# The last layer norm of a decoder layer, moved beside the last expert of a mixture of experts

## The chip, the cores and the metric

The kernel runs on one core of a Trainium2 chip. The metric is the device time of one execution in microseconds (us), lower is better. Every time of the profile below comes from one profiled execution, and its clock starts with that execution's first instruction.

## The reference

One decoder layer over 1024 tokens of width 1024, all float32. The first half (windowed attention, a convolution branch, a gated merge, a layer norm) is not touched by the change. What follows it is:

```
h     = layer_norm(alpha * x + mix)                       # 1024 x 1024
logits = h @ w_router + b_router;  top 4 of 32 experts, softmax over the 4
for each chosen expert e:  up = h @ w_up[e] + b_up[e]      # 1024 -> 2048
    act = min(up[::2],7) * sigmoid(1.702*...) * (clip(up[1::2],-7,7) + 1)
    y_moe += gate * (act @ w_down[e] + b_down[e])          # 1024 -> 1024
out   = layer_norm(alpha * h + y_moe) * ln2_g + ln2_b
```

## The kernel before

**Experts.** The 32 experts are ranked by their number of tokens. Rank j has a fixed capacity `CAPS[j]` (320 slots for rank 0, 256 for rank 5, 64 for ranks 25 to 31). Tokens above a capacity go to a list that a loop at the end works off, in chunks of 128 (`nxv` chunks; with these inputs there are none). Two DRAM tensors hold the state of a token: `hd` has h, and `yd` starts as alpha*h plus the gated b_down and collects the experts' rows. An expert gathers its rows of `hd` by index, and scatters its gated result into `yd` with an indirect DMA that adds (`scatter`, line 319, on GpSimd's queue). Two scatters are never in flight at once, since both write `yd`.

**Blocks.** A capacity is cut in blocks of 128 slots, and one of 64 or 32. For a 128-block every float32 product is three matmuls over high and low parts (line 251), and the weights are split into these parts on ScalarE and VectorE (`split`, lines 86 and 87). For a block of 64 slots, 64 columns of the array serve each half of the outputs (line 260): its result lies as 128 partitions x 512, in which slot t has its first 512 channels in partition t and the others in partition 64 + t. `si` holds the row index of such half rows.

**Steps and pairs.** An expert takes 12 steps: 0 to 3 and 4 to 7 are the two halves of the up projection, 8 to 11 the down projection. Each step needs 1 MB of weights, loaded on SP's queue into 24 slots of 512 KB; a planner (`fits`) issues a load as soon as the slots allow. The experts are taken in pairs, and the two of a pair alternate by phases of four steps. The last pair is rank 5 (256 slots, tiles named `p5...`) and rank 25 (64 slots, `p25...`). The order of the steps is the list G:

```
G = [(e, 4 * ph + s) for pair in pairs for ph in range(3) for e in pair for s in range(4)]
```

What goes with a step (transposes, SwiGLU, bias, scatter, gathers) is entered in a table with `at(step, function)`, and `behind(g)` issues it after the matmuls of step g, in a fixed order of kinds. Each engine works off its instructions in the order in which they were issued. Accumulators in PSUM come from 5 buffers; a 128-block needs two of them in a phase, a 64-block one.

**The end.** After the last step come the remaining entries of the table, then the loop over overflow chunks (`nxv`, lines 1328 and 1329), and then the last layer norm: eight tiles `fy` of 128 tokens are loaded from `yd` on SP's queue (line 1358), and for each one VectorE takes statistics (`fst`, `fmv`), ScalarE a square root, and the normalisation is shared between VectorE (line 1377), ScalarE (1381) and GpSimd (1382):

```
nc.vector.scalar_tensor_tensor(y[:, cs], y[:, cs], mv[:, 0:1], LG2[0][:, cs], op0=ALU.subtract, op1=ALU.mult)
if b == NB - 1 or c == 1:
    nc.vector.scalar_tensor_tensor(y[:, cs], y[:, cs], rstd, LG2[1][:, cs], op0=ALU.mult, op1=ALU.add)
else:
    nc.scalar.activation(y[:, cs], y[:, cs], AF.Copy, scale=rstd)
    nc.gpsimd.tensor_tensor(y[:, cs], y[:, cs], LG2[1][:, cs], op=ALU.add)
```

Of the kernel before, what the change touches and what calls it, by code (L numbers as in the profile page):

```python
# [53 lines left out]
PAIRS = [(6, 31), (1, 30), (13, 19), (2, 29), (9, 14), (7, 20), (21, 22), (0, 28), (15, 23), (3, 27), (10, 16), (8, 24),  # L54
         (11, 17), (4, 26), (12, 18), (5, 25)]
TR = 9 * P


@with_exitstack
def kernel(ctx: ExitStack, tc: tile.TileContext, x, w_in, b_in, attn_sinks, w_attn_br,  # L60
# [36 lines left out]
    def trp(name):  # L97
        return ps.tile([P, 512], F32, name=name, tag="tr", bufs=3)
# [1079 lines left out]
    with tc.manual_schedule():  # L1178
        NS = 12
        pairs = [(ex[n], ex[n + 1]) for n in range(0, NE, 2)]  # L1180
        G = [(e, 4 * ph + s) for pair in pairs for ph in range(3) for e in pair for s in range(4)]
        total = len(G)
        pos = {(e.pfx, s): g for g, (e, s) in enumerate(G)}

# [38 lines left out]
        def overflow():  # L1223
# [12 lines left out]
            for d in (1, 2, 4, 8, 16):  # L1236
# [19 lines left out]
            nc.sync.dma_start(xti[:, :], xci)  # L1256


        todo = {}

        rank_of = ("x_T", "swiglus", "act_T", "scale_out", "bias_of", "scatter", "fetch", "indices", "gather", "load_row",
                   "load_bias")

        def at(g, f, *a):
            todo.setdefault(g, []).append((f, a))
# [2 lines left out]
        g0 = {e.pfx: pos[e.pfx, 0] for e in ex}  # L1268
        tpos = [g0[e.pfx] - 2 - e.nb + i for e, i in blocks]
        for n, e in enumerate(ex):  # L1270
            p = g0[e.pfx] - 4 * (n % 2)
            if n > 1:
                at(p - 16, e.fetch)
                at(p - 13, e.indices)
# [8 lines left out]
            for i in range(e.nb):  # L1283
                at(pos[e.pfx, 4 + i], e.act_T, 0, i)
                at(pos[e.pfx, 8 + (i > 0)], e.act_T, 1, i)
                at(pos[e.pfx, 11], e.scale_out, i)
            at(pos[e.pfx, 11] + 2, e.scatter)
        for n, (e, i) in enumerate(blocks):
            if n >= XG:
                f = g0[e.pfx] // 24 * 24  # L1290
# [26 lines left out]
        for g, (e, s) in enumerate(G):  # L1317
# [3 lines left out]
                overflow()  # L1321
            load_ahead(g)
            behind(g)
        for g in sorted(todo):
            behind(g)


    nxv = nc.values_load(nxi[0:1, 0:1], min_val=0, max_val=NPX)  # L1328
    with tc.For_i(0, nxv, 1) as it:  # L1329
        xe = mo.tile([1, 2], I32, name="xe", tag="xe")  # L1330
        nc.sync.dma_start(xe, xti[bass.ds(it, 1), :])
        ev = {n: n.value_load(xe[0:1, 0:1], min_val=0, max_val=NE - 1) for n in (nc.sync, nc.gpsimd)}
        row = nc.gpsimd.value_load(xe[0:1, 1:2], min_val=0, max_val=NE * TR - P)
        idx = [mo.tile([P, 4, 2], F32, name="xm", tag="xm"), mo.tile([P, 4], I32, name="xgi", tag="xgi"), None]
        e = Expert("x", P, lambda eng=nc.sync: ev[eng], idx, fast=False)
        e.fetch(row)
        e.indices()
        e.gather(0)
        e.x_T(0)
        for s in range(12):  # L1340
            e.load(s)
            e.mm(s)
            if s in (3, 7):
                for u in (s // 2 - 1, s // 2):
                    e.load_row(u)
                    e.bias_of(u)
                e.swiglus(s // 4)
                e.act_T(s // 4, 0)
        e.scale_out(0)
        e.scatter()  # L1350


    mctx.close()
    fin = ctx.enter_context(tc.tile_pool(name="fin", bufs=2, reuse_waits="tile"))
    FY, LG2 = [], []
    for b in range(NB):
        FY.append(fin.tile([P, D], F32, name=f"fy{b}", tag="fy", bufs=8))
        nc.sync.dma_start(FY[b], yd[b * P:(b + 1) * P, :])
        if b < 2:
            row = fin.tile([1, D], F32, name=f"l2row{b}", tag=f"l2row{b}", bufs=1)  # L1360
            nc.scalar.dma_start(row, (ln2_g, ln2_b)[b])
            bc = fin.tile([P, D], F32, name=f"l2bc{b}", tag=f"l2bc{b}", bufs=1)
            nc.gpsimd.partition_broadcast(bc, row)
            LG2.append(bc)
    for b in range(NB):
        y = FY[b]
        mv = fin.tile([P, 2], F32, name=f"fmv{b}", tag="fmv")
        st = fin.tile([P, 2, 6], F32, name=f"fst{b}", tag="fst")
        for h in range(2):
            nc.vector.bn_stats(st[:, h, :], y[:, h * 512:(h + 1) * 512])  # L1370
        nc.vector.bn_aggr(mv, st)  # L1371
        rstd = fin.tile([P, 1], F32, name=f"frs{b}", tag="frs")
        nc.scalar.activation(rstd, mv[:, 1:2], AF.Sqrt, bias=eps_t)  # L1373
        nc.vector.reciprocal(rstd, rstd)  # L1374
        for c in range(2) if b >= NB - 2 else (None,):
            cs = slice(None) if c is None else slice(c * 512, (c + 1) * 512)
            nc.vector.scalar_tensor_tensor(y[:, cs], y[:, cs], mv[:, 0:1], LG2[0][:, cs], op0=ALU.subtract, op1=ALU.mult)  # L1377
            if b == NB - 1 or c == 1:
                nc.vector.scalar_tensor_tensor(y[:, cs], y[:, cs], rstd, LG2[1][:, cs], op0=ALU.mult, op1=ALU.add)  # L1379
            else:  # L1380
                nc.scalar.activation(y[:, cs], y[:, cs], AF.Copy, scale=rstd)  # L1381
                nc.gpsimd.tensor_tensor(y[:, cs], y[:, cs], LG2[1][:, cs], op=ALU.add)  # L1382
            (nc.scalar if b % 2 else nc.sync).dma_start(out[b * P:(b + 1) * P, cs], y[:, cs])  # L1383


_INS = ['x', 'w_in', 'b_in', 'attn_sinks', 'w_attn_br', 'conv_w', 'conv_b', 'conv_ln_g', 'conv_ln_b', 'w_conv_br',
# [25 lines left out]
```

## Time and profile before

| | us |
|---|---|
| median of 3 runs | 2189.25 (2187.02 to 2190.99) |
| the profiled execution | 2188.17 |
| its span, first to last instruction | 2186.6 |
| matmuls of the last pair, first to last | 2038.3 to 2129.4 |
| loop over overflow chunks left | 2139.9 |
| last layer norm on VectorE | 2143.65 to 2177.8 |

The span and the time of the execution differ by 1.57 us. The mean granted clock of TensorE is 0.976 of full speed; the stretch after the last matmul has most of what is missing.

### The profile page before, as it was taken

How to read it: one execution, taken by the hardware profiler on the slowest of the kernel's cores; microseconds unless marked ns; L12 is line 12 of the kernel's file. 1: busy time of each engine (PE TensorE's matmuls, PEld its weight loads, DVE VectorE, ACT ScalarE, POOL GpSimd, SP SyncE). 2: the span in 40 equal slices, each digit the busy share in tenths (PEclk: the TensorE clock that was granted, in tenths of full speed). 3: DMA queues.
4: the chain of work that ended last, by engine and by line, in shares of the span. 5: the costliest groups of instructions: out<-in, count | busy, mean ns of one | idle time of the engine just before them, and what ended most of it. 6: DMA issues, size and time to landing. Idle time of an engine off the chain costs nothing. (4 is left out here: it accounts for less than half of the span.)

```text
span 2186.6 us, 31962 instructions
## 1 busy us (share of the span) xinstructions
PE 2069.1 (95%) x10925; PEld 1370.3 (63%) x10925; DVE 1377.5 (63%) x2052; ACT 878.9 (40%) x1337; POOL 496.8 (23%) x643
## 2 busy tenths in 40 slices
PE   8999999999959999999999999989999999999990
PEld 7776788887635566576654355556676466766760
DVE  3768799665845564656964126365596569569635
ACT  3155511432323433435653123334455357356521
POOL 1000000003332222323241322122243241232204
PEclk9999999999979999999999999999999999999995
DMA  5111112142339988998998997899889898988944
GB/s 161 41 37 30 30 49 58 34 139 64 107 116 326 313 289 301 362 347 266 319 312 296 345 333 259 283 335 328 281 312 285 307 305 303 357 259 314 346 161 162
DMA packets 191096, 506.92 MB, mean 232 GB/s; under 512 B 34700, under 2 KB 70974, under 8 KB 190929
## 3 DMA queue, kind: packets, MB, share of 16 engines
q1 hardware_dynamic: 163062, 448.86, 57.9%
q0 software_dynamic: 26592, 52.21, 9.9%
q10 hardware_dynamic: 1275, 3.77, 0.4%
q8 instruction: 87, 1.43, 0.3%
q14 instruction: 80, 0.66, 0.1%
HBM read 471.26 MB, written 33.49 MB: 231 GB/s over the span
## 5 line engine op out<-in xcount | busy, mean ns | idle before, releaser
L600 DVE SCALAR_TENSOR_TENSOR c<-a,cw,c 128x1024 f32<-128x1024 f32 x120 | 154.0, 1284 | 3.3
L828 POOL DMA_DIRECT2D bu<-in_b_up_dram x2 | 1.0, 502 | 456.4 <-DVE wol L87 456.4
L139 POOL DMA_DIRECT2D slt<-tab x103 | 54.5, 530 | 26.3 <-issue 12.5
L90 PE MATMUL ga<-xh,whga 128*128 128x512 f32 x128 | 52.1, 407 | 0.0
L92 PE MATMUL ga<-xh,wlga 128*128 128x512 f32 x128 | 50.5, 395 | 0.0
L91 PE MATMUL ga<-xl,whga 128*128 128x512 f32 x128 | 50.5, 394 | 0.0
L92 PE MATMUL gb<-xh,wlgb 128*128 128x512 f32 x128 | 50.4, 394 | 0.0
L90 PE MATMUL gb<-xh,whgb 128*128 128x512 f32 x128 | 50.4, 394 | 0.0
L91 PE MATMUL gb<-xl,whgb 128*128 128x512 f32 x128 | 50.4, 394 | 0.0
L1021 POOL DMA_INDIRECT tab<-rec,dst x32 | 32.7, 1021 | 59.5 <-DMA tab<-rec,dst 58.3
L927 PE MATMUL wo<-woh,mh 128*128 128x512 f32 x128 | 37.1, 424 | 0.6 <-ACT mh L86 0.6
L87 DVE TENSOR_TENSOR p8l<-p8w,p8h 128x1024 fp32r<-128x1024 f32 x24 | 29.5, 1281 | 10.3 <-ACT p8h L86 6.3
L927 PE MATMUL wo<-woh,ml 128*128 128x512 f32 x128 | 35.9, 404 | 0.0
L87 DVE TENSOR_TENSOR p7l<-p7w,p7h 128x1024 fp32r<-128x1024 f32 x24 | 29.3, 1270 | 9.8 <-ACT p7h L86 9.7
L927 PE MATMUL wo<-wol,mh 128*128 128x512 f32 x128 | 35.0, 409 | 0.0
L441 ACT ACTIVATE gt<-ga,pcol 128x512 f32<-128x512 f32 x16 | 11.0, 690 | 59.2 <-PE ga L92 59.1
L643 DVE SCALAR_TENSOR_TENSOR sc<-s,mask 128x512 f32<-128x512 f32 (+1 forms) x32 | 19.5, 652 | 23.9 <-PE s L640 21.8
L87 DVE TENSOR_TENSOR p0l<-p0w,p0h 128x1024 fp32r<-128x1024 f32 x24 | 29.6, 1270 | 7.4 <-ACT p0h L86 7.1
L87 DVE TENSOR_TENSOR p11l<-p11w,p11h 128x1024 fp32r<-128x1024 f32 x24 | 29.8, 1295 | 4.8 <-ACT p11h L86 4.6
L87 DVE TENSOR_TENSOR p1l<-p1w,p1h 128x1024 fp32r<-128x1024 f32 x24 | 28.5, 1241 | 5.0 <-ACT p1h L86 4.8
L87 DVE TENSOR_TENSOR p15l<-p15w,p15h 128x1024 fp32r<-128x1024 f32 x24 | 27.9, 1219 | 5.6 <-issue 4.7
L87 DVE TENSOR_TENSOR p13l<-p13w,p13h 128x1024 fp32r<-128x1024 f32 x24 | 27.9, 1219 | 5.4 <-ACT p13h L86 5.2
(1240 smaller groups left out, 6381.8 us busy)
## 6 DMA issues: line engine op xcount, KB each, us to landing
p6w<-in_w_up_dram SPq DMA_DIRECT2D x16, 512.0 KB
p31w<-in_w_up_dram SPq DMA_DIRECT2D x16, 512.0 KB
p1w<-in_w_up_dram SPq DMA_DIRECT2D x16, 512.0 KB
p30w<-in_w_up_dram SPq DMA_DIRECT2D x16, 512.0 KB
p13w<-in_w_up_dram SPq DMA_DIRECT2D x16, 512.0 KB
p19w<-in_w_up_dram SPq DMA_DIRECT2D x16, 512.0 KB
p2w<-in_w_up_dram SPq DMA_DIRECT2D x16, 512.0 KB
p29w<-in_w_up_dram SPq DMA_DIRECT2D x16, 512.0 KB
```

What stands on the lines that cost most here:

```text
L87: nc.vector.tensor_tensor(lo, src, hi.bitcast(F32), op=ALU.subtract)
L90: nc.tensor.matmul(o, ah, bh, start=start, stop=False)
L91: nc.tensor.matmul(o, ah, bl, start=False, stop=False)
L92: nc.tensor.matmul(o, al, bh, start=False, stop=stop)
L139: nc.gpsimd.dma_start(self.m[g * w:(g + 1) * w, i, :], tab[bass.ds(row + c, w), :])
L441: nc.scalar.activation(GT[c][:, sl], t, AF.Sigmoid, bias=bin_c(14 + c))
L600: nc.vector.scalar_tensor_tensor(C[c], A[c][:, w:w + S], cw[:, c, w:w + 1], C[c], op0=ALU.mult, op1=ALU.add)
L643: nc.vector.scalar_tensor_tensor(SC[b][c0 // 2][:, g::2, :W], t[g][:, :, :W], 0.125, mk[:, None, :].to_broadcast([P, 2, W]), op0=ALU.mult, ...
L828: nc.gpsimd.dma_start(bu, b_up[:, i * S:(i + 1) * S])
L927: nc.tensor.matmul(t, ml[:, k, :], W[k][:, sl], start=n == 0, stop=n == 3 * KC - 1)
L1021: nc.gpsimd.indirect_dma_start(out=tab[:, :], out_offset=bass.IndirectOffsetOnAxis(ap=DST[b][:, k:k + 1], axis=0), in_=REC[:, b, k, :], in ...
```

## The change

Rank 5 and rank 25 no longer alternate: all 12 steps of rank 5 come first, then the 12 of rank 25. Rank 5 scatters right after its last step. During rank 25's steps the kernel loads all of `yd` (which lacks rank 25's share alone) in eight tiles, on GpSimd's queue, normalises them and stores them to `out`. In six of the eight tiles the sums come from ScalarE (Copy and Square with accumulated outputs), in two (`FDVE`) from VectorE; both passes of the normalisation are on VectorE. The rows of rank 25's tokens are wrong in this store. They are done apart: `fin_gather` fetches the half rows of `yd` for its slots, `fin_slots` adds the expert's result and normalises them in slot order (two small matmuls bring together the statistics of both halves), and `fin_scatter` writes them over the rows in `out`, without adding. The overflow loop is now inside a branch that is taken only if there are chunks; it then scatters rank 25 into `yd`, works off the chunks, and does the layer norm once more.

```diff
+FDVE = (0, 4)
-        G = [(e, 4 * ph + s) for pair in pairs for ph in range(3) for e in pair for s in range(4)]
+        G = [(e, 4 * ph + s) for pair in pairs[:-1] for ph in range(3) for e in pair for s in range(4)]
+        G += [(e, s) for e in pairs[-1] for s in range(NS)]
+        last = ex[-1]
+        FY, F = {}, {}
+        HALVES = (slice(0, 512), slice(512, 1024))
+        in_halves = lambda ap: ap.rearrange("t (c d) -> (t c) d", c=2)
+        def fin_const():
+            for i, ap in enumerate((ln2_g, ln2_b)):
+                t = F["w", i] = mo.tile([P, D], F32, name=f"l2w{i}", tag="xg", bufs=XG)
+                nc.gpsimd.dma_start(t, ap.to_broadcast([P, D]))
...
+            F["s"] = mo.tile([P, 4, NB], F32, name="f_s", tag="f_s", bufs=1)
+        def fin_gather():
+            F["y"] = mo.tile([P, 512], F32, name="yg", tag="ys64", bufs=2)
+            nc.gpsimd.indirect_dma_start(out=F["y"], out_offset=None, in_=in_halves(yd),
+                                         in_offset=bass.IndirectOffsetOnAxis(ap=last.si[:, 0:1], axis=0))
+        def fin_load(b, tag, pfx="fy"):
+            FY[b] = mo.tile([P, D], F32, name=f"{pfx}{b}", tag=tag, bufs=1 if tag[0] == "W" else 2)
+            nc.gpsimd.dma_start(FY[b], yd[b * P:(b + 1) * P, :])
+        def fin_stats(b, dve=False):
+            y, s = FY[b], F["s"][:, :, b:b + 1]
+            if dve:
+                st = mo.tile([P, 2, 6], F32, name=f"fst{b}", tag="fst")
+                for h, sl in enumerate(HALVES):
+                    nc.vector.bn_stats(st[:, h, :], y[:, sl])
+                mv = mo.tile([P, 2], F32, name=f"fmv{b}", tag="fmv")
+                nc.vector.bn_aggr(mv, st)
+                nc.vector.tensor_scalar(s[:, 1], mv[:, 0:1], -1.0, None, op0=ALU.mult)
+                nc.vector.tensor_scalar(s[:, 2], mv[:, 1:2], float(D), None, op0=ALU.mult)
+            else:
+                for i, f in enumerate((AF.Copy, AF.Square)):
+                    o = mo.tile([P, D], F32, name=f"fo{b}{i}", tag="ys128")
+                    if i == 0:
+                        nc.scalar.activation(o, y, AF.Copy, accum_out=s[:, 0])
+                        nc.scalar.activation(s[:, 1], s[:, 0], AF.Copy, scale=-1.0 / D)
+                    else:
+                        nc.scalar.activation(o, y, AF.Square, bias=s[:, 1], accum_out=s[:, 2])
+            nc.vector.scalar_tensor_tensor(y, y, s[:, 1], F["w", 0], op0=ALU.add, op1=ALU.mult)
+        def fin_out(*bs):
+            s = F["s"][:, :, bs[0]:bs[-1] + 1]
+            nc.scalar.activation(s[:, 3], s[:, 2], AF.Sqrt, bias=eps_t, scale=1.0 / D)
+            nc.vector.reciprocal(s[:, 3], s[:, 3])
+            for b in bs:
+                y = FY.pop(b)
+                nc.vector.scalar_tensor_tensor(y, y, F["s"][:, 3, b:b + 1], F["w", 1], op0=ALU.mult, op1=ALU.add)
+                nc.sync.dma_start(out[b * P:(b + 1) * P, :], y)
+        def fin_slots():
+            y = F["y"]
+            nc.vector.scalar_tensor_tensor(y, last.acc[0][0], last.m[:, 0, 1:2], y, op0=ALU.mult, op1=ALU.add)
...             (statistics of 512, two matmuls over the halves, a square root, two passes of 512)
+        def fin_scatter():
+            nc.gpsimd.indirect_dma_start(out=in_halves(out), out_offset=bass.IndirectOffsetOnAxis(
+                ap=last.si[:, 0:1], axis=0), in_=F["y"], in_offset=None, bounds_check=2 * S - 1, oob_is_err=False)
...
+        q = pos[last.pfx, 0]
+        at(q - 3, fin_const)
+        at(q, fin_gather)
+        for b in range(NB):
+            at(q, fin_load, b, ("xh128", "xl128", "ah128", "al128")[b // 2])
+        for s, b in zip((4, 5, 6, 7, 8, 9, 10, 11), range(NB)):
+            at(q + s, fin_stats, b, b in FDVE)
+        for s, bs in ((7, (0, 1)), (8, (2, 3)), (9, (4, 5)), (11, (6, 7))):
+            at(q + s, fin_out, *bs)
...
+        fin_slots()
+        fin_scatter()
+        last.scale_out(0)
     nxv = nc.values_load(nxi[0:1, 0:1], min_val=0, max_val=NPX)
-    with tc.For_i(0, nxv, 1) as it:
+    with tc.If(nxv > 0):
+        last.scatter()
+        with tc.For_i(0, nxv, 1) as it:
...             (the body of the loop, unchanged)
+        for b in range(NB):
+            fin_load(b, f"W{b}", "ry")
+            fin_stats(b, True)
+            fin_out(b)
-    (the loads, statistics and passes of the last layer norm described above, 30 lines)
```

## Rows read from the trace of the kernel before

**Rows 1.** The page's first part: busy us, share of the span, instructions.

```profile
PE 2069.1 (95%) x10925; PEld 1370.3 (63%) x10925; DVE 1377.5 (63%) x2052; ACT 878.9 (40%) x1337; POOL 496.8 (23%) x643
```

**Rows 2.** Busy time by stretch: length, PE, PEld, DVE, ACT, POOL, clock, DMA share, GB/s.

```profile
2038.00:2061.00 23.00, 23.00 (x107) 18.58 (x105) 9.05 (x13) 6.72 (x9) 8.71 (x12) 1.00 1.04 370
...
2129.50:2139.90 10.40, 0.00 (x0) 0.00 (x0) 0.00 (x0) 0.66 (x1) 1.55 (x1) 0.64 0.52 76
...
2143.60:2177.80 34.20, 0.00 (x0) 0.00 (x0) 31.10 (x45) 9.64 (x15) 19.83 (x9) 0.50 0.51 203
...
2180.00:2186.60 6.60, 0.00 (x0) 0.00 (x0) 0.00 (x0) 0.00 (x0) 0.00 (x0) 0.50 0.00 0
```

**Rows 3.** The chain that ended last, 2127 to 2144: start us, us, what.

```profile
2127.34 1.57 DMA yd<-p5ys,gi
...
2134.30 4.86 DMA yd<-p25ys,si
...
2139.87 3.76 DMA fy<-yd
```

**Rows 4.** Timeline of TensorE, last pair: start, us, line, op, tiles, count.

```profile
2061.05 7.09 PE L260 MATMUL p25u<-p25w,p25xr 128*64 128x512 f32 x32
...
2121.74 1.94 PE L260 MATMUL p25d<-p25w,p25ar 128*64 128x512 f32 x8
...
2124.05 5.37 PE L260 MATMUL p25d<-p25w,p25ar 128*64 128x512 f32 x24
```

**Rows 5.** Timeline of GpSimd: a gather, a scatter; in brackets the idle time before.

```profile
2003.97 1.15 POOL L152 DMA_INDIRECT p25xg<-hd,gi  x1 [0.31 <-issue]
...
2120.11 1.65 POOL L319 DMA_INDIRECT yd<-p5ys,gi  x1 [56.75 <-ACT p5ys L315]
```

**Rows 6.** The tensor yd: ns min/median/max of a scatter, first and last start.

```profile
L319 POOL DMA_INDIRECT yd<-p19ys,si x2: 1568/1924/2281, 931.4 to 940.9; - x2
...
L319 POOL DMA_INDIRECT yd<-p21ys,si x2: 1597/1643/1689, 1275.6 to 1286.5; - x2
L319 POOL DMA_INDIRECT yd<-p22ys,si x2: 1580/1622/1665, 1295.5 to 1302.4; - x2
```

**Rows 7.** GpSimd's issue of plain scatters and of a 512 KB DMA, ns min/median/max.

```profile
L1021 POOL DMA_INDIRECT tab<-rec,dst x32: 960/971/1422, 539.3 to 647.8; - x32
...
L530 POOL DMA_DIRECT2D yd<-zt x1: 544/544/544, 13.1 to 13.1; - x1
```

**Rows 8.** The chain in the last layer norm, GpSimd not at work yet.

```profile
2150.63 0.56 DVE fst L1370
2151.18 1.19 DVE fy L1377
```

**Rows 9.** Timeline of VectorE: the SwiGLU of rank 5's four accumulators.

```profile
2057.83 0.69 DVE L270 TENSOR_TENSOR p5t<-p5u,p5bc 128x512 f32<-128x512 f32 x1 [11.54 <-POOL p5bc L225]
2058.55 0.30 DVE L274 TENSOR_SCALAR p5t<-p5t 128x256 f32<-128x256 f32 x1
...
2065.53 0.43 DVE L276 SCALAR_TENSOR_TENSOR p5act<-p5sg,p5t 128x256 f32<-128x256 f32 x1
```

**Rows 10.** ScalarE's prices: by tile, ns min/median/max, or by line, busy us, mean ns.

```profile
L772 ACT ACTIVATE sq<-c x4: 1041/1042/1061, 392.1 to 395.0; 128x1024 f32<-128x1024 f32 x4
...
L1373 ACT ACTIVATE frs<-fmv,eps_t x8: 278/294/295, 2145.2 to 2172.2; 128x1 f32<-128x1 f32 x8
...
L1373 ACT ACT_TABLE_LOAD x1 | 1.3, 1283 | 10.6 <-DMA l2row<-in_ln_g_dram 10.6
```

**Rows 11.** The program's last line: the sequencers' own instructions, ns min/median/max.

```profile
L1408 POOLq DRAIN  x3: 52/115/13810, 2171.9 to 2186.3; - x3
```

**Rows 12.** Timeline of ScalarE at the moment of rows 9.

```profile
2058.55 0.44 ACT L272 ACTIVATE p5sg<-p5t 128x256 f32<-128x256 f32 x1 [7.91 <-DVE p5t L270]
```

**Rows 13.** Timeline of the last layer norm: GpSimd and VectorE together.

```profile
2155.93 13.50 POOL L1382 TENSOR_TENSOR fy<-fy,l2bc 128x1024 f32<-128x1024 f32 x5 [10.12 <-issue]
2156.13 3.21 DVE L1377 SCALAR_TENSOR_TENSOR fy<-fy,fmv,l2bc 128x1024 f32<-128x1024 f32 x1
```

More of the change, by code (lines that the diff above doesn't have):

```diff
@@ L1256, in overflow @@
             nc.sync.dma_start(xti[:, :], xci)
+        last = ex[-1]
+        assert [w for w, c in last.blocks] == [64]
+        FY, F = {}, {}
[5 more added lines that the diff above has]
+                nc.gpsimd.dma_start(t, ap.to_broadcast([P, D]))
+            for i, ap in enumerate((ln2_g, ln2_b)):
+                t = F["h", i] = mo.tile([P, 512], F32, name=f"l2h{i}", tag="bc", bufs=BC)
+                for h, sl in enumerate(HALVES):
+                    nc.gpsimd.dma_start(t[h * 64:(h + 1) * 64], ap[:, sl].to_broadcast([64, 512]))
+            av, df = (mo.tile([P, P], F32, name=n, tag=n, bufs=1) for n in ("f_av", "f_df"))
+            for h in range(2):
+                nc.vector.tensor_tensor(av[:, h * 64:(h + 1) * 64], ident[:, 0:64], ident[:, 64:128], op=ALU.add)
+            nc.vector.tensor_scalar(av, av, 0.5, None, op0=ALU.mult)
+            nc.vector.tensor_tensor(df, ident, av, op=ALU.subtract)
+            F["av"], F["df"] = av, df
+            F["s"] = mo.tile([P, 4, NB], F32, name="f_s", tag="f_s", bufs=1)
@@ L1270 @@
         for n, e in enumerate(ex):
-            p = g0[e.pfx] - 4 * (n % 2)
+            p = g0[e.pfx] // 24 * 24
             if n > 1:
@@ L1285 @@
                 at(pos[e.pfx, 8 + (i > 0)], e.act_T, 1, i)
-                at(pos[e.pfx, 11], e.scale_out, i)
-            at(pos[e.pfx, 11] + 2, e.scatter)
+                if e is not last:
+                    at(pos[e.pfx, 11], e.scale_out, i)
+            if e is not last:
+                at(pos[e.pfx, 11] + (0 if e is ex[-2] else 2), e.scatter)
+        q = pos[last.pfx, 0]
[7 more added lines that the diff above has]
+            at(q + s, fin_out, *bs)
         for n, (e, i) in enumerate(blocks):
@@ L1323 @@
             behind(g)
-        for g in sorted(todo):
-            behind(g)
+        assert not todo
+        fin_slots()
+        fin_scatter()
+        last.scale_out(0)
     nxv = nc.values_load(nxi[0:1, 0:1], min_val=0, max_val=NPX)
-    with tc.For_i(0, nxv, 1) as it:
[L1330 to L1350, printed above, removed]
@@ L1353 @@
-    mctx.close()
[L1354 to L1383, printed above, removed]
+    with tc.If(nxv > 0):
+        last.scatter()
+        with tc.For_i(0, nxv, 1) as it:
+            xe = mo.tile([1, 2], I32, name="xe", tag="xe")
+            nc.sync.dma_start(xe, xti[bass.ds(it, 1), :])
+            ev = {n: n.value_load(xe[0:1, 0:1], min_val=0, max_val=NE - 1) for n in (nc.sync, nc.gpsimd)}
+            row = nc.gpsimd.value_load(xe[0:1, 1:2], min_val=0, max_val=NE * TR - P)
+            idx = [mo.tile([P, 4, 2], F32, name="xm", tag="xm"), mo.tile([P, 4], I32, name="xgi", tag="xgi"), None]
+            e = Expert("x", P, lambda eng=nc.sync: ev[eng], idx, fast=False)
+            e.fetch(row)
+            e.indices()
+            e.gather(0)
+            e.x_T(0)
+            for s in range(12):
+                e.load(s)
+                e.mm(s)
+                if s in (3, 7):
+                    for u in (s // 2 - 1, s // 2):
+                        e.load_row(u)
+                        e.bias_of(u)
+                    e.swiglus(s // 4)
+                    e.act_T(s // 4, 0)
+            e.scale_out(0)
+            e.scatter()
+        for b in range(NB):
+            fin_load(b, f"W{b}", "ry")
+            fin_stats(b, True)
+            fin_out(b)
```

17 lines of the change are left out of this document (16 added, 1 removed).

## The prediction

> **What bounds the kernel now.** I read the page first, then the busy time by stretch over the last 150 us, then the chain that ended last, then the timeline of each engine there. The page says that TensorE is busy for 95% of the span [rows 1], so until its last matmul nothing but fewer matmuls, or fewer gaps, would help, and this change removes none. The stretches show where the other 5% sit: while the last pair runs, TensorE is busy without a gap at full clock, from 2038.3 on; after 2129.4 it does nothing for 57 us [rows 2]. The reader should see this tail as a serial chain. Rank 5's second scatter, then rank 25's scatter, then the first load of `yd`, each waiting for the landing of the one before [rows 3]; then 34.2 us in which VectorE is busy for 31.1; then 6.6 us in which no engine and no DMA does anything [rows 2]. Only this tail can shrink.
>
> What bounds the new kernel is the same kind of chain, started earlier: rank 5's last matmul, its scatters, the loads, the layer norm, and then a short finish for 64 slots. I put it on the clock of the execution before.
>
> **Rank 5's last matmul: 2106.9.** TensorE's work of the pair stays the same, but rank 25's three phases move behind it. They take 7.1, 7.7 and 7.7 us (32 matmuls each; the later two, of which the last runs from 2121.74 to 2129.42, hold two transposes as well) [rows 4], together 22.5: 2129.4 - 22.5 = 2106.9. The un-alternated order could cost gaps. The planner keeps loads 8 steps ahead of use in either order (counted through its rule), and rank 5's steps of 5.6 us each need a load of 2.8 us (1 MB at the 370 GB/s of [rows 2]), so weights are not late. I take no gap; the accumulators are a rival below. Moving the pair's first transposes and biases by some steps costs nothing, since TensorE's queue covers them; if it didn't, they are under 1 us each.
>
> **The scatters: rank 25's rows can be read at 2121.8.** The first scatter starts 1.6 us before the last matmul (2120.11 against 2121.74 [rows 4, 5]), so at 2105.3. Before, it had the DMA engines to itself, and the second began 7.2 us later [rows 3, 5]. Now rank 25's last loads run beside it: the last four steps' weights are issued from two steps before the end on, which is DMA work until about 2116. Twelve pairs of scatters stand in the trace, most of them beside loads: their distances run from 6.9 to 10.9 us, with a middle of 9.5 [rows 6] (the three shown: 9.5, 10.9, 6.9). I take 9.5 for the first and 7.0 for the second (2127.34 to 2134.30 [rows 3]), together 16.5. Bounds: 13.9 and 20.4. The `fin_const` loads (1.5 MB) stand ahead of these scatters in GpSimd's queue, but 15 us earlier, when the DMA engines have room.
>
> **The first tile: 2127.3.** Behind the scatters GpSimd issues the gather, 1.15 us [rows 5], and a load, 0.54 [rows 7]. The load of 512 KB took 3.76 us to arrive when SP issued it [rows 3]. Sum 5.5. These loads move from SP's queue to GpSimd's. The Trainium skill, in DMA: Bandwidth & Descriptors, section Anatomy of one DMA — SWDGE (gpsimd) path, fits GpSimd's DMAs with 2.0 us plus the bytes at 436 GB/s; by it the estimate is 3.2 us in place of 3.76, and the whole 0.6 us shorter. Bounds from rows: 5 and 8 (gather and load with the 2.3 us of the longest issue in [rows 6]). The other seven follow at about 1.4 us each (512 KB at the rate above), ahead of their use.
>
> **The layer norm of all tokens: 31 us, to 2158.3.** Now all passes are VectorE's: 16 of 128x1024 at 1.19 us each in a row, as long as GpSimd does nothing [rows 8], 19.0. Two tiles have VectorE's statistics, two of 0.56 [rows 8], their aggregate and two tiny ones: 1.6 each, 3.2. Rank 25's second SwiGLU stands in the same queue behind the third tile, 2.0 (four of this size took from 2057.83 to 2065.96 [rows 9]). Four reciprocals, 0.4. Then the waits: a tile of ScalarE's needs a Copy, a tiny op and a Square, 1.05 + 0.29 + 1.05 [rows 10], with the reading out of two sums some 2.6 us, and the pass that overwrites the tile must wait for the Square. VectorE waits about 1.3 us for each of the tiles 1 and 2; for tile 3, whose sums stand behind the SwiGLU's sigmoid, 1.9; and 0.4 for the first square root, which has a table load of 1.28 before it [rows 10]. From tile 4 on ScalarE is ahead. Waits 4.9; some fifteen handoffs of 0.1. Sum 31. Bounds: 29.5 with no handoffs, 34 if ScalarE stays behind at tiles 5 to 7 as well (1.3 each). Rank 25's own matmuls don't bind: the SwiGLU ends some 10 us after the first tile, four steps at most remain, 7.2 us, and even twice that is over before VectorE is. So TensorE will stand idle for some 13 us in rank 25's second half, at no price.
>
> **The slots: 4.5 us, to 2162.8.** In a row on VectorE: the sum with the accumulator 0.7, statistics 0.6, their aggregate 0.15, two small matmuls with both handoffs 0.9, three tiny ones 0.35, two passes of 512 at 0.7, handoffs 0.4. The square root hides behind the first pass. The scatter needs the stores of all tiles landed too; the last is issued at 2158.3 and needs 3 to 4 us, just hidden. If it isn't, it costs 1 us.
>
> **The last scatter: landed at 2167.5.** Rank 25's adding scatter took 4.86 us [rows 3]; this one doesn't add, and GpSimd's plain scatters issue in 0.97 instead of 1.6 [rows 7]. I take 4.7, bounds 3.4 and 4.9.
>
> **The branch and the end: 2174.8.** The loop was left 0.7 us after the scatter had landed (2139.16 to 2139.87 [rows 3]); I take the same for the branch, and up to 3 more if branch and loop each wait. The end is 6.6 us behind the last byte of the stores (no DMA from 2180.0 on [rows 2]), and GpSimd's drain lasts from 2171.9 to 2185.7 [rows 11]. I take the distance from the landing, 5.7, and 0.9 behind it; whether it counts from there isn't shown. Bounds: nothing beyond 0.9, and 8.
>
> **The sum.** 2186.6 - 2174.8 = 11.8 us less. The profiled execution (2188.17) is 1.1 below the median; from the median 2189.25 - 11.8 = 2177.5 us, 0.54% faster. Less of the layer norm lies beside rank 25's matmuls than the words of the change suggest: these last 22.5 us, and the first tile arrives 20.4 us after their start. What is won is rank 25's scatter and load, and its matmuls, which now pass while rank 5's scatters land.
>
> **The rivals.** *ScalarE and VectorE take turns.* All statistics lie in one small tile that both write. Were its columns not told apart, each Copy would wait for the pass before: 4.0 us a ScalarE tile, six times, 2.8 for the others, 3 for each of four outputs, the SwiGLU; some 45 instead of 31, and the time 2191.5. Against it: ScalarE reads the even columns of `p5t` in the same moment in which VectorE writes its odd ones [rows 9, 12]. Chance 0.10, no measurable change. *The accumulators.* Without rank 25's phase in between, rank 5 needs four of five buffers right after four. The SwiGLU frees them until 2066 [rows 9], 5 us into the next phase; if TensorE waited for all, twice, 9.5 us and 2187. Against it: it starts 3.2 us before the phase ends, and each buffer is freed by its first instruction, 2 us before it is needed. Chance 0.07, no change. *VectorE slowed by GpSimd*, the other side. Beside GpSimd's additions a pass took 3.21 us instead of 1.19 [rows 13]. If GpSimd's DMA work did the same to all 16 passes, 32 us more, 2209; it decides from 1 us a pass on (11.8 plus 4.4 over 16). Against it: GpSimd issues its eight loads before the first pass, and then nothing until the last scatter. The Trainium skill, in SBUF — State Buffer, section SBUF: two separate sides, has a port pair that VectorE and GpSimd lock against each other for a whole instruction; by that rule the passes lengthen only beside a GpSimd instruction that reads SBUF, which agrees with [rows 13]. Chance 0.07, slower. *A shorter end.* If scatters and drain come at their lower bounds (2.6 + 5.7 less), 2169 to 2172. For it: the drain's cause is unknown. Chance 0.16.
>
> **How the numbers follow.** 0.60 for the forecast, whose own range from its bounds is 2173 to 2184. About 0.2%, 4.4 us, is what a measurement of this kernel can tell from no change. Faster: 0.60 and 0.16, less 0.01 for the forecast's upper edge, 0.75. Same: 0.17. Slower: 0.07, and 0.01 from the turns, 0.08. For the range I leave out the slow rival, the turns and the lowest end: 2170.5 to 2188.
>
> **What would show it.** In the new profile: no gap in rank 5's matmuls; its scatters 8 to 11 and then 7 us apart; the first tile's statistics 20 us after rank 5's last matmul; passes of 1.2 us; 31 us until the last of them; then 4.5 us, the scatter, and an end 11 to 13 us after its start. I would be wrong if ScalarE's Copy of a tile starts only behind a VectorE pass, if passes take over 2 us, or if TensorE shows gaps inside rank 5.

## The result and the profile after

| | before | after |
|---|---|---|
| median of 4 runs each, one chip, us | 2188.34 (2187.02 to 2190.99) | 2171.6 (2170.8 to 2174.53) |
| profiled execution, us | 2188.17 | 2172.18 |
| its span, us | 2186.6 | 2170.6 |

The change makes the kernel faster: ratio 0.9927, 95% interval 0.9913 to 0.9941, that is 16.7 us of the median (13 to 19), where 11.8 were forecast. The time lies in the predicted range, but below the likeliest case's own (2173 to 2184): it lies in the band of the rival called a shorter end (2169 to 2172).

TensorE's share on the page's first part is that of [rows 1], so its work has not changed (in all rows, PE is TensorE, PEld its weight loads, DVE VectorE, ACT ScalarE, POOL GpSimd, and a q behind the name stands for the engine's sequencer):

```profile
PE 2065.7 (95%) x10929; PEld 1368.4 (63%) x10929; DVE 1373.6 (63%) x2049; ACT 887.2 (41%) x1357; POOL 487.9 (22%) x649
```

The busy time by stretch (columns as in [rows 2]) covers the pair and the tail:

```profile
2039.20:2062.00 22.80, 22.80 (x102) 18.87 (x101) 14.71 (x18) 10.10 (x12) 5.96 (x8) 1.00 1.03 367
2062.00:2085.00 23.00, 23.00 (x107) 19.13 (x106) 18.34 (x27) 10.68 (x14) 4.07 (x7) 1.00 0.81 266
2085.00:2107.50 22.50, 22.50 (x108) 18.28 (x106) 9.94 (x18) 8.39 (x12) 2.63 (x3) 1.00 0.74 253
...
2128.30:2160.10 31.80, 7.87 (x26) 2.37 (x26) 25.28 (x35) 18.11 (x37) 2.06 (x4) 0.61 0.55 213
2165.10:2168.00 2.90, 0.00 (x0) 0.00 (x0) 0.00 (x0) 0.00 (x0) 1.04 (x1) 0.50 0.25 93
2168.00:2170.60 2.60, 0.00 (x0) 0.00 (x0) 0.00 (x0) 0.00 (x0) 0.00 (x0) 0.50 0.00 0
```

Rank 5's three phases are the first three rows, and TensorE has no gap in them. The serial tail of [rows 3] is still there, but starts 14 us earlier, as GpSimd's timeline shows:

```profile
2105.91 1.69 POOL L320 DMA_INDIRECT yd<-p5ys,gi  x1 [19.00 <-ACT p5ys L316]
2116.67 1.58 POOL L320 DMA_INDIRECT yd<-p5ys,gi  x1 [9.07 <-ACT p25sg L273]
...
2123.19 1.02 POOL L1287 DMA_INDIRECT yg<-yd,si  x1 [3.74 <-DMA yd<-p5ys,gi]
2124.21 1.65 POOL L1292 DMA_DIRECT2D fy<-yd  x3
2127.75 2.61 POOL L1292 DMA_DIRECT2D fy<-yd  x5 [1.89 <-issue]
2165.13 1.04 POOL L1344 DMA_INDIRECT out_dram<-yg,si  x1 [34.76 <-DVE yg L1341]
```

The two scatters stand 10.8 us apart, then the gather and the loads follow, and at the end the last scatter. VectorE's timeline between them (statistics of tile 0, the passes of tiles 1 to 3 with the waits, the last passes, the slots):

```profile
2128.26 1.29 DVE L1300 BATCH_NORM_STATS2 fst<-fy 128x6 f32<-128x512 f32 x2 [11.57 <-DMA fy<-yd]
...
2134.02 1.28 DVE L1313 SCALAR_TENSOR_TENSOR fy<-fy,f_s,l2w 128x1024 f32<-128x1024 f32 x1 [2.73 <-ACT fo L1312]
2136.58 1.28 DVE L1313 SCALAR_TENSOR_TENSOR fy<-fy,f_s,l2w 128x1024 f32<-128x1024 f32 x1 [1.27 <-ACT fo L1312]
...
2141.52 1.28 DVE L1313 SCALAR_TENSOR_TENSOR fy<-fy,f_s,l2w 128x1024 f32<-128x1024 f32 x1 [1.74 <-ACT fo L1312]
...
2157.64 2.48 DVE L1321 SCALAR_TENSOR_TENSOR fy<-fy,f_s,l2w 128x1024 f32<-128x1024 f32 x2
2160.04 0.74 DVE L1327 SCALAR_TENSOR_TENSOR yg<-p25d,slt,yg 128x512 f32<-128x512 f32 x1
...
2164.09 0.75 DVE L1341 SCALAR_TENSOR_TENSOR yg<-yg,fss,l2h 128x512 f32<-128x512 f32 x1
```

VectorE waits for ScalarE's sums at tiles 1 to 3 and never again; all passes take 1.28 us in the records, 1.20 from start to start. ScalarE's own first row says why the first of these waits is the longest, namely that tile 1 reached it only at 2131.3, 3 us behind tile 0:

```profile
2131.33 1.06 ACT L1309 ACTIVATE fo<-fy 128x1024 f32<-128x1024 f32 x1 [13.60 <-DMA fy<-yd]
```

The rows of GpSimd's sequencer in the last lines stand against [rows 11]; the DRAIN is the instruction with which an engine ends the program:

```profile
L1431 POOLq INC_SWDGE_SEM  x1: 451/451/451, 2168.1 to 2168.1; - x1
L1484 POOLq DRAIN  x3: 56/109/1127, 2168.6 to 2170.3; - x3
```

GpSimd's drain lasts 1.1 us where it lasted 13.8. The last scatter has landed when the first of these rows starts, at 2168.1 (the stretch behind it has no DMA), and 2.5 us later the program is over; before, the last 6.6 us passed without DMA [rows 2].

### The profile page after: what moved, and what is told of

Read it like the earlier page. It is cut to its first block, busy times and chain, and to the rows that moved or that the text cites. A ratio compares the mean times of both kernels' runs of the same rounds, so it can differ in the third digit from the quotient of the medians.

```text
span 2170.6 us, 31922 instructions
## 1 busy us (share of the span) xinstructions
PE 2065.7 (95%) x10929; PEld 1368.4 (63%) x10929; DVE 1373.6 (63%) x2049; ACT 887.2 (41%) x1357; POOL 487.9 (22%) x649
## 3 DMA queue, kind: packets, MB, share of 16 engines
q0 software_dynamic: 28240, 58.23, 10.8%
## 5 line engine op out<-in xcount | busy, mean ns | idle before, releaser
L88 DVE TENSOR_TENSOR p5l<-p5w,p5h 128x1024 fp32r<-128x1024 f32 x24 | 29.0, 1242 | 9.8 <-ACT p5h L87 9.2
```

Source lines behind the costliest of these rows:

```text
L88: nc.vector.tensor_tensor(lo, src, hi.bitcast(F32), op=ALU.subtract)
```

## The experiments

Twelve kernels ran. Each ratio is against executions of the kernel before on the same chip, taken together with it (medians 2186.9, 2186.9, 2183.6 and 2186.0 us). Executions differ in all that stands ahead: rank 5's first scatter started at 2101.14 to 2109.30 in the eleven profiled executions with the new order. So the table also gives the tail of each profiled execution: from the start of that scatter to the last instruction. With the new order all of rank 25's matmuls lie behind that scatter, so tails compare only among kernels of one order; the old one have "before", "additions on VectorE" and "before, loads on GpSimd".

| kernel | median, us | ratio (95%) | tail, us | long drain at the end |
|---|---|---|---|---|
| before | | | 66.5 | 13.8 |
| after | 2171.6 | 0.9927 (0.9913 to 0.9941) | 64.7 | no, 1.1 |
| order only | 2180.57 | 0.9972 (0.9960 to 0.9983) | 77.2 | 13.8 |
| additions on VectorE | 2181.37 | 0.9972 (0.9960 to 0.9983) | 57.3 | 11.2, early |
| both | 2177.62 | 0.9958 (0.9944 to 0.9973) | 69.0 | 11.5, early |
| layer norm behind the loop | 2170.16 | 0.9923 (0.9907 to 0.9940) | 62.7 | no, 1.1 |
| loads on SP | 2181.47 | 0.9973 (0.9963 to 0.9983) | 73.8 | 10.4 |
| one load on GpSimd | 2179.53 | 0.9972 (0.9962 to 0.9982) | 72.8 | 10.4 |
| after, an addition on GpSimd | 2168.58 | 0.9915 (0.9896 to 0.9935) | 65.6 | no, 1.1 |
| loads on SP, the addition | 2176.11 | 0.9964 (0.9950 to 0.9978) | 73.2 | 10.4 |
| before, loads on GpSimd | 2186.82 | 1.0012 (1.0002 to 1.0021) | 69.3 | 24.5 |
| behind the loop, tiles 0 and 1 on VectorE | 2166.5 | 0.9911 (0.9890 to 0.9931) | 56.7 | no, 1.1 |
| the same, half of the loads on SP | 2162.29 | 0.9897 (0.9881 to 0.9914) | 55.5 | no, 0.8 |
| the same, three loads on GpSimd | 2167.05 | 0.9910 (0.9893 to 0.9926) | 57.9 | no, 0.7 |

To compare across the orders, the clock is started at rank 5's first matmul, whose work on TensorE is the same in all kernels. These are its rows in the five kernels of the table below, in that order:

```profile
2038.33 0.39 PE L251 MATMUL p5u<-p5h,p5xh 128*128 128x512 f32 x1
2037.27 0.39 PE L251 MATMUL p5u<-p5h,p5xh 128*128 128x512 f32 x1
2043.03 0.39 PE L251 MATMUL p5u<-p5h,p5xh 128*128 128x512 f32 x1
2041.20 0.39 PE L251 MATMUL p5u<-p5h,p5xh 128*128 128x512 f32 x1
2039.23 0.39 PE L252 MATMUL p5u<-p5h,p5xh 128*128 128x512 f32 x1
```

| us from rank 5's first matmul to | rank 25's scatter into `yd` | first statistics of the layer norm | last instruction |
|---|---|---|---|
| before | 96.0 | 105.3 | 148.3 |
| order only | 92.4 | 101.7 | 143.8 |
| additions on VectorE | 95.9 | 105.3 | 139.1 |
| both | 92.4 | 101.7 | 135.7 |
| after | none | 89.0 | 131.4 |

### Which part brings the gain

**Order only.** The kernel before with the un-alternated last pair and rank 5's entries of the table placed to match.

```diff
-        G = [(e, 4 * ph + s) for pair in pairs for ph in range(3) for e in pair for s in range(4)]
+        G = [(e, 4 * ph + s) for pair in pairs[:-1] for ph in range(3) for e in pair for s in range(4)]
+        G += [(e, s) for e in pairs[-1] for s in range(NS)]
...
-            p = g0[e.pfx] - 4 * (n % 2)
+            p = g0[e.pfx] // 24 * 24
```

> The kernel before with the un-alternated order of the last pair alone; the layer norm stays behind the loop. My theory: rank 25's 22.5 us of matmuls now pass while rank 5's two scatters land, so its own scatter starts when its result is ready (2130.4 on the clock of before) and not at 2134.3: 3.9 us less, about 2184.5. Rival (the order itself costs TensorE gaps, 5 us twice, since rank 5 needs its accumulators at once): 2188 to 2192. Rival (no part of the gain comes from the order): 2188.3.

Measured 2180.57, 6.3 us less (3.7 to 8.7). GpSimd's timeline of this kernel:

```profile
2103.95 1.65 POOL L319 DMA_INDIRECT yd<-p5ys,gi  x1 [40.38 <-ACT p5ys L315]
2115.10 1.57 POOL L319 DMA_INDIRECT yd<-p5ys,gi  x1 [9.49 <-DMA yd<-p5ys,gi]
2129.66 1.55 POOL L319 DMA_INDIRECT yd<-p25ys,si  x1 [12.99 <-ACTq L1330]
...
2150.53 13.51 POOL L1383 TENSOR_TENSOR fy<-fy,l2bc 128x1024 f32<-128x1024 f32 x5 [9.95 <-issue]
```

Rank 5's scatters come 16 and 12 us earlier than in [rows 3, 5], but rank 25's only 4.6 (2129.66 against 2134.30), and 1.1 of these are the earlier start of the pair: from rank 5's first matmul the scatter comes 3.6 us earlier, near the 3.9 that were expected. It now waits for rank 25's last matmuls. From there to the end 51.4 us pass, 52.3 before. The median's other 2 to 3 us are not in the tail, and may be noise in what stands ahead.

**Additions on VectorE.** The kernel before with the last layer norm's additions moved off GpSimd.

```diff
-                nc.gpsimd.tensor_tensor(y[:, cs], y[:, cs], LG2[1][:, cs], op=ALU.add)
+                nc.vector.tensor_tensor(y[:, cs], y[:, cs], LG2[1][:, cs], op=ALU.add)
```

> The kernel before with the layer norm's additions moved from GpSimd to VectorE, nothing else. Theory: GpSimd's additions have three prices in the tail: GpSimd starts the first one 10 us after it is free, VectorE's passes beside them take up to 3.2 us, and the drain at the end lasts 5.7 us beyond the landing of the stores. Without them VectorE needs 8 tiles of 3.85 us, 31 instead of 34.2, the passes take 1.2, and the end follows the last byte by 2.6 us instead of 7.2: about 7.5 us less, 2181. Rival (the drain has nothing to do with the additions): the end stays 7 us, 3 us less, 2185. Rival (GpSimd's share was worth having): 2188 or more.

Measured 2181.37, 5.5 us less (3.7 to 8.7). The drain is not gone, but is now recorded from 2148.7 on, at the broadcasts and beside VectorE's work, and is over 22 us ahead of the end. Its rows, behind rank 25's scatter:

```profile
2138.91 1.55 POOL L319 DMA_INDIRECT yd<-p25ys,si  x1 [5.41 <-issue]
...
L1408 POOLq DRAIN  x3: 52/115/11160, 2148.7 to 2181.9; - x3
```

From that scatter to the end 43.2 us pass, 52.3 before (2134.30 to 2186.6). Of the 9.1 us, 3.5 are a shorter layer norm on VectorE (30.6 us against 34.1) and 5.7 what comes behind it (3.1 us against 8.8).

**Both edits together**, and the layer norm still behind rank 25's scatter.

> The kernel before with two small edits only: the last pair not alternated, and the last layer norm's additions on VectorE in place of GpSimd; the layer norm still stands behind rank 25's scatter. Alone they gave 6.3 and 5.5 us on the same chip. If they add up, 2175, which leaves 3 to 5 us of the change for the slots that are finished apart. If what the change gains comes from the layer norm standing beside rank 25's steps, the two together give little more than one alone: 2179 to 2181.

Measured 2177.62, 9.3 us less. The median lies between the two expectations; the interval (5.9 to 12.2 us) holds the sum, 11.8, and also the order alone, 6.3. The profile decides for the sum. These are rank 5's first scatter and rank 25's:

```profile
2107.87 1.66 POOL L319 DMA_INDIRECT yd<-p5ys,gi  x1 [40.38 <-ACT p5ys L315]
...
2133.58 1.55 POOL L319 DMA_INDIRECT yd<-p25ys,si  x1 [13.92 <-ACTq L1330]
```

Between them 25.7 us pass, as with the order alone (2103.95 to 2129.66), and from there to the end 43.3, as with the additions alone (43.2). Against the kernel after, which has the same order, the tail is 4.3 us longer (69.0 and 64.7). After starts its layer norm 12.6 us earlier than this kernel (89.0 against 101.7 us from rank 5's first matmul), but gives most of it back: its norm takes 1.3 us longer, and behind the norm it still has 10.5 us to go (slots, scatter, end) where this kernel has 3.5.

**Layer norm behind the loop.** The kernel after with statistics and passes issued in the same order, but behind all of rank 25's steps.

```diff
-        for s, b in zip((4, 5, 6, 7, 8, 9, 10, 11), range(NB)):
-            at(q + s, fin_stats, b, b in FDVE)
-        for s, bs in ((7, (0, 1)), (8, (2, 3)), (9, (4, 5)), (11, (6, 7))):
-            at(q + s, fin_out, *bs)
...
+        for b in range(NB):
+            fin_stats(b, b in FDVE)
+            for n, bs in ((3, (0, 1)), (4, (2, 3)), (5, (4, 5)), (7, (6, 7))):
+                if n == b:
+                    fin_out(*bs)
```

> The changed kernel, but the statistics and passes of the eight tiles are issued behind all steps of rank 25, in the same order; loads and scatters stay. Theory: the first tile arrives only 21 us after rank 5's last matmul, when rank 25's matmuls would be nearly over, so the layer norm isn't beside the expert anyway; what stands in its queue is rank 25's second SwiGLU, 2.0 us and the 1.7 us that tile 3 waits behind it. Out of the queue: 3.7 us less than the changed kernel, about 2168. TensorE then ends near 2131, with no idle stretch of 15 us. Rival (the place beside the expert's steps is what the change gains by): 2.5 to 10 us more, 2174 to 2181.

Measured 2170.16, with an interval that nearly covers that of after; the tail is 2.0 us shorter, and the drain stays at 1.1. So the norm's place among rank 25's steps brings nothing: the loads can't start before rank 5's scatters have landed, and once rank 25's SwiGLU stands ahead of the norm, its last matmul ends at 2131.3, 5 us behind the first statistics:

```profile
2124.21 7.07 PE L261 MATMUL p25d<-p25w,p25ar 128*64 128x512 f32 x24
...
2126.09 1.29 DVE L1300 BATCH_NORM_STATS2 fst<-fy 128x6 f32<-128x512 f32 x2 [2.43 <-DMA fy<-yd]
```

There is little left to stand beside.

### What sets the end

**Loads on SP.** The kernel after with `fin_load` on SP's queue, as the layer norm of before had it.

```diff
-            nc.gpsimd.dma_start(FY[b], yd[b * P:(b + 1) * P, :])
+            nc.sync.dma_start(FY[b], yd[b * P:(b + 1) * P, :])
```

> The changed kernel with the eight loads of yd on SP's queue instead of GpSimd's. Theory: the loads then don't stand behind the gather and its issue, so the first tile's statistics start 1.0 to 1.5 us earlier, and all that follows: about 2170.3. Rival (SP holds them back behind its weight loads): later first tile, 2172 or more.

This missed by 11 us: 2181.47. The loads did come sooner (3.9 us from the gather's start to the first statistics, 5.1 in after), and the last scatter started at 2162.68, 2.45 us ahead of after's. Then the end grew:

```profile
L1431 POOLq INC_SWDGE_SEM  x1: 2717/2717/2717, 2165.6 to 2165.6; - x1
L1484 POOLq DRAIN  x3: 56/109/10362, 2168.3 to 2179.3; - x3
```

For 10.4 us, from 2168.3 on, no engine and no DMA does anything while GpSimd drains, and the instruction ahead of it (INC_SWDGE_SEM) has grown from 0.45 to 2.7 us. This is an end like that of [rows 2, 11], here without any addition or broadcast on GpSimd in the tail. The Trainium skill, in DMA: Bandwidth & Descriptors, section SWDGE vs HWDGE vs iDMA, sends plain transfers to SP's or ScalarE's queue and leaves accumulating and irregular ones to GpSimd; for the loads this run agrees (they came 1.2 us sooner behind the gather), for the kernel it cost 9.1 us of tail against after.

**One load on GpSimd.** The kernel after with the last tile's load on GpSimd's queue and the other seven on SP's.

```diff
-            nc.gpsimd.dma_start(FY[b], yd[b * P:(b + 1) * P, :])
+            (nc.gpsimd if b == NB - 1 else nc.sync).dma_start(FY[b], yd[b * P:(b + 1) * P, :])
```

> The kernel after with seven of the eight loads of yd on SP's queue and the eighth on GpSimd's, which issues it right behind the gather. With all eight on SP's the drain was 10.4 us and the time 2181.5. Theory that a single plain load behind the gather already does what the eight do: drain near 1.1 us, and as the first tiles come earlier by SP the time is about 2169. Rival, that it takes several of them (GpSimd paused 1.9 us between its third and fourth load): drain about 10 us and 2181 again.

Measured 2179.53, with a drain of 10.4: one load is too few.

**After, with an addition on GpSimd**, 24 us ahead of the last scatter.

```diff
+        def fin_add():
+            o = mo.tile([P, 512], F32, name="f_add", tag="f_add", bufs=1)
+            nc.gpsimd.tensor_tensor(o, F["w", 0][:, 0:512], F["w", 1][:, 0:512], op=ALU.add)
...
+        at(q + 8, fin_add)
```

> The kernel after, with one elementwise addition on GpSimd (128x512 into a tile that nothing reads) put beside rank 25's ninth step, behind the eight loads and long before the last scatter; the output is the same. Open is what makes GpSimd's drain at the end last 13.8 us before and 10.4 with the loads on SP's queue, but 1.1 after. Theory that a change of the kind of GpSimd's work costs some 10 us (before has 10.1 us of 'issue' between its last broadcast and its first addition): the addition brings it back, the drain lasts about 10 us, or the last scatter is late by as much, time about 2180. Rival, that it hangs on which transfers GpSimd has issued since its scatters: the drain stays near 1.1 us and the time at 2171.6.

Measured 2168.58. Each of the two theories got one half right. GpSimd's rows of that line, and the drain:

```profile
L1326 POOLq MODIFY_POOL_CONFIG  x2: 37/37/37, 2126.5 to 2126.6; - x2
L1326 POOL TENSOR_TENSOR f_add<-l2w,l2w x1: 1258/1258/1258, 2135.9 to 2135.9; 128x512 f32<-128x512 f32 x1
...
L1489 POOLq DRAIN  x3: 56/109/1127, 2165.2 to 2166.9; - x3
```

Here a change to elementwise work does cost GpSimd 9.4 us: its configuration is changed at 2126.5 (MODIFY_POOL_CONFIG), the addition's operands have long been there, and it starts at 2135.9. But the drain at the end stays short. The Trainium skill, in GPSIMD Engine Reference, section 2.1 Instruction dispatch, counts about 6 us for the first call to a freshly loaded GpSimd kernel, seen behind MODIFY_POOL_CONFIG and with no instruction of its own in the profile. The traces have such a stall at that place; in before it is 6.8 us early in the program (below) and 10.1 in the last layer norm.

```profile
L868 POOLq MODIFY_POOL_CONFIG  x2: 127/127/127, 505.5 to 505.5; - x2
...
512.36 0.14 POOL L868 IOTA prt<- 128x1 f32 x1 [6.82 <-issue]
```

**Loads on SP, and the addition.**

> The kernel after with the eight loads on SP's queue (drain 10.4 us, 2181.5) and, on GpSimd, the one addition of 128x512 beside rank 25's ninth step (with the loads on GpSimd it started 9.4 us late, and the drain stayed at 1.1). Theory that GpSimd has one piece of some 10 us to do after its scatters, at the first occasion, which is the addition here: the addition starts some 10 us late, long before the end, the drain is about 1 us, and the time is about 2169. Rival, that the addition's late start and the long drain are two things: the drain is again 10 us or more, 2181.

Measured 2176.11, 5 us under the rival's time, but with the rival's drain. The 5 us lie ahead of the tail: in this kernel and in the one before, the two with the added tile, rank 5's first scatter came 4 us earlier (2101.14 and 2101.63) than in the loads on SP and in after (2105.74 and 2105.91), for a reason that these runs don't show.

```profile
L1326 POOL TENSOR_TENSOR f_add<-l2w,l2w x1: 1257/1257/1257, 2131.1 to 2131.1; 128x512 f32<-128x512 f32 x1
its engine sat idle before it (us, times) until:
  issue: 11.8, 1
...
L1489 POOLq DRAIN  x3: 56/109/10362, 2163.1 to 2174.0; - x3
```

The addition is 11.8 us late, the drain is long all the same, and the tail (73.2) is that of the loads on SP. So the stall ahead of an addition doesn't spare the drain.

**Before, with the loads on GpSimd.** The eight loads of the kernel before on GpSimd's queue, in their places.

```diff
-        nc.sync.dma_start(FY[b], yd[b * P:(b + 1) * P, :])
+        nc.gpsimd.dma_start(FY[b], yd[b * P:(b + 1) * P, :])
```

> The kernel before with nothing changed but the queue of the eight loads of yd at the end: GpSimd's in place of SP's, in the same places of the program. Its drain was 13.8 us, of which 9.8 lie behind GpSimd's last addition, and ended the execution. Theory that GpSimd's own transfers ahead of the end make the drain short, whatever else GpSimd does: drain gone within about 1 us of the last addition, the end follows the last store, some 6 us less, 2180 to 2181. Rival, that GpSimd's additions make the drain long in any case: 2186 to 2189.

Measured 2186.82, ratio 1.0012: the rival's. GpSimd's additions and its drain:

```profile
2157.38 18.27 POOL L1382 TENSOR_TENSOR fy<-fy,l2bc 128x1024 f32<-128x1024 f32 x7 [12.35 <-ACT fy L1381]
...
L1408 POOLq DRAIN  x3: 52/115/24527, 2161.6 to 2186.7; - x3
```

The last addition ended at 2175.7, and the drain, recorded from 2161.6 beside the additions, 10.5 us later (2161.6 + 24.5). So loads ahead of the additions do nothing for the drain behind them.

### A faster version

**Two tiles on VectorE.** On top of the layer norm behind the loop: VectorE's own statistics for tiles 0 and 1 in place of 0 and 4, and tile 0's second pass right behind its first.

```diff
-FDVE = (0, 4)
+FDVE = (0, 1)
...
-            for n, bs in ((3, (0, 1)), (4, (2, 3)), (5, (4, 5)), (7, (6, 7))):
+            for n, bs in ((0, (0,)), (2, (1,)), (3, (2, 3)), (5, (4, 5)), (7, (6, 7))):
```

> The kernel after with the layer norm issued behind the loop (as in the run before with that change, 2170.2) and with VectorE's own statistics for tiles 0 and 1 in place of 0 and 4, tile 0's second pass moved ahead of tile 1: VectorE then works while ScalarE, which gets its first tile about 4 us after VectorE gets the first, makes the sums of tiles 2 to 7. VectorE's waits for tiles 1 to 3 (2.9, 1.3, 1.3, 0.3 us) should fall to under 1 us in all and the layer norm from 30 to some 25 us; the end follows at once, if it hangs on the last scatter: about 2165. If the drain becomes long for any reason: 2175 or more.

Measured 2166.5. The layer norm took 24.4 us (2127.80 to 2152.17) where it took 29.6, with one wait left of 0.35, and the tail fell from 62.7 to 56.7.

**Half of the loads on SP**, on top of it: tiles 0 to 3 there, 4 to 7 on GpSimd's queue.

```diff
-            nc.gpsimd.dma_start(FY[b], yd[b * P:(b + 1) * P, :])
+            (nc.sync if b < 4 else nc.gpsimd).dma_start(FY[b], yd[b * P:(b + 1) * P, :])
```

> The fastest kernel so far (layer norm behind the loop, VectorE's statistics for tiles 0 and 1, 2166.5) with the loads of tiles 0 to 3 on SP's queue and those of tiles 4 to 7 on GpSimd's. Eight loads on GpSimd's queue left a drain of 1.1 us, one or none left 10.4. Theory that some number of GpSimd's own transfers decides, reached with the fourth (its pause of 1.9 us fell between the third and the fourth): drain 1.1, the first tile about 0.5 us earlier, time 2165 to 2166.5. Rival, that it takes more than four: drain about 10 us, time 2175.

Measured 2162.29, ratio 0.9897: 21 us less than before, the lowest median here, though its interval overlaps that of the kernel above; the tail is 1.2 us shorter. Between the gather's start and the first statistics lie 3.3 us (2126.11 to 2129.43) where there were 5.1. The drain is 0.8, so four loads on GpSimd's queue do what eight do.

**Three loads on GpSimd**, tile 4's moved to SP's queue as well (`b < 5`).

> The fastest kernel so far (four loads on SP's queue, four on GpSimd's, 2162.3, drain 0.8 us) with tile 4's load moved to SP's queue as well, so that GpSimd issues three. In every run with a short drain GpSimd paused 1.8 to 1.9 us ahead of its fourth load; the runs with none or one load had no pause and a drain of 10.4. Theory that the fourth load, the one behind the pause, is what spares the drain: without it the drain is about 10 us again, and the time about 2172. Rival, that two or three loads do: drain about 1 us, no loss, 2162 to 2163.

Measured 2167.05, with a drain of 0.7: the theory of the fourth load falls. GpSimd's timelines, first with four loads, then with three, there with VectorE's last pass:

```profile
2127.13 1.65 POOL L1292 DMA_DIRECT2D fy<-yd  x3
2130.72 0.53 POOL L1292 DMA_DIRECT2D fy<-yd  x1 [1.94 <-PE p25d L261]
2159.42 1.04 POOL L1344 DMA_INDIRECT out_dram<-yg,si  x1 [28.17 <-SPq L1432]
```

```profile
2127.05 1.64 POOL L1292 DMA_DIRECT2D fy<-yd  x3
...
2158.88 0.75 DVE L1341 SCALAR_TENSOR_TENSOR yg<-yg,fss,l2h 128x512 f32<-128x512 f32 x1
...
2162.01 1.04 POOL L1344 DMA_INDIRECT out_dram<-yg,si  x1 [33.33 <-issue]
```

With four, the pause of 1.9 us stands ahead of the fourth load, where nobody waits. With three, the next transfer is the last scatter: VectorE had its rows ready at 2159.63 (2158.88 and 0.75), and GpSimd started at 2162.01, 2.4 us later. With four it started 0.3 us behind VectorE (2159.13 and 2159.42). So a pause on the path accounts for most of the 2.4 us by which the tails differ (57.9 and 55.5). It stands ahead of the fifth transfer from the gather on, load or scatter, and in this kernel after 33 us in which GpSimd issued nothing; of the kernels with the new layer norm, those with five or more have a short drain, those with two or three a long one. All of them issue the same transfers ahead of the gather, and the first four make the same 1.75 MB, so whether a number or an amount counts is not shown, nor what two loads would do.

## Why the prediction was right, and where it was off

On the profiled executions the span fell by 16.0 us; 11.8 were forecast. The steps in order; "later" is against the clock of the forecast:

- **Rank 5's last matmul**, 2106.9: rank 25's first starts at 2107.54. There is no gap, so the rival of the accumulators is out. It is 0.6 later, less than the 0.9 by which the pair started later (2039.23 against 2038.33).
- **The scatters**, 9.5 and 7.0: 10.8 and 6.5 (2105.91, 2116.67, 2123.19). The first shares the DMA engines with rank 25's weights as forecast (DMA share 1.04 until the second starts) and was taken 1.3 too short; it stayed inside the bounds. The twelve pairs behind the 9.5 are those of two blocks of one kind; the nine distances in the same trace from a 128-block's scatter to that of the same expert's smaller block run from 9.8 to 12.2, so the spread was wider than the forecast saw.
- **The first tile**, 5.5: 5.07 from the gather's start to the statistics. The estimate by the Trainium skill's page DMA: Bandwidth & Descriptors (section Anatomy of one DMA — SWDGE (gpsimd) path), 4.9, was 0.2 off, that by the row 0.4.
- **The layer norm**, 31: 31.9 (2128.26 to 2160.12), with waits of 2.7, 1.3, 1.7 and 0.3 us, 6.1 instead of 4.9 (the last one for the first square root). The long one is tile 1's: its load landed 3 us behind tile 0's, where 1.4 were forecast. ScalarE's Copy of tile 2 (2133.90 to 2134.94) runs beside VectorE's pass over tile 1 (from 2134.02), so the rival of the turns is out, and with passes at 1.20 from start to start the one of a slowed VectorE too. TensorE stood idle for 15.6 us in rank 25's second half, where 13 were forecast, at no price.
- **The slots**, 4.5: 5.0 to the scatter's start. The two small matmuls took 0.56 each, at a granted clock of 0.50 (1.2 GHz), 14 us behind the matmul before them.
- **The landing, the branch and the end**, 12.0 from the scatter's start: 5.5. This is the term that was mis-sized, by 6.5 us; all others together are 2.3 long, and the difference, 4.2, is what the forecast missed. The landing took 3.0 instead of 4.7, and behind it came 2.5 instead of 7.3. So the errors partly cancelled by luck: with the end as forecast, the gain would have been 9.5.

The mechanism was right: a serial tail, started some 14 us earlier. What failed is the sentence "I take the distance from the landing, 5.7". The 5.7 us were no distance from a landing; they were what was left of GpSimd's drain, which ended at 2185.7 [rows 11], 9.8 us behind its last addition:

```profile
2171.32 4.57 POOL L1382 TENSOR_TENSOR fy<-fy,l2bc 128x1024 f32<-128x1024 f32 x2 [1.89 <-ACT fy L1381]
```

The forecast had named the drain and given "nothing beyond 0.9" as the lower bound, and had put 0.16 on a shorter end. Of that rival only the end came; the scatters, which it had 2.6 shorter, were 0.8 longer. That the drain was at stake is shown: with the additions on VectorE it lies beside other work, and what comes behind the layer norm shrinks by 5.7 us; with the loads on SP it returns, at 10.4 us, and takes about 11 of the 16.7 us with it.

The forecast also said where the gain does not come from, and this held: the norm can stand behind rank 25's steps at no loss. From rank 5's first matmul on, three parts add up to it: the order brings rank 25's scatter 3.6 us forward, the additions give 9.1 by leaving GpSimd (the drain behind them and VectorE's slower passes beside them), and the rest of the change 4.3. The sum, 17.0, agrees with the 16.9 by which that stretch fell and with the 16.7 of the medians. The 4.3 are one number for all the rest: the slots finished apart, the sums on ScalarE, the queue of the loads and the branch were not tried one by one against the kernel with both edits. The single edits' medians, 6.3 and 5.5, fit this less well, since they hold the noise of what stands ahead.

Left open: what GpSimd does in these 10 us. The runs show when the drain is long, not why. That a short drain hangs on the transfers issued from the gather on fits the runs with the new layer norm; the kernel before with its loads on GpSimd, which has eight and then additions, shows that something done later brings it back.

## What to carry to other kernels

Read the end of a kernel as a chain of its own: when the last bytes land, which engine's drain ends last, and what that engine did before; here a few plain loads on the queue of the free engine were worth more than the faster queue. Two small edits that a profile suggests (an order, an engine for an addition) gave over half of what the large change gave, so make them first and alone. When a second engine supplies sums, let the consumer make the first ones itself until the supplier is ahead.

## What the runs showed of the hardware

- GpSimd stalls without a wait that the profile shows when it goes from broadcasts or transfers to elementwise work: 6.8 us early in before, 10.1 in its last layer norm, and 9.95, 9.4 and 11.8 us in three experiments. The drain behind such work at the end lasts as long again (9.8 and 10.5 us behind the last addition).
- The drain takes 10.4 us with no such work as well, where GpSimd issued only a gather, up to one load and a scatter behind the adding scatters and two small bias loads; with three or more loads it took 0.7 to 1.1. The instruction ahead of it (INC_SWDGE_SEM) goes with it: 2.7 us and 0.35 to 0.45.
- A pause of 1.8 to 2.4 us stands ahead of the fifth transfer from that gather on, be it a load or, after 33 us without a transfer, a scatter.
